# Scan groups in pairs on TensorE, one visit for the transposes of the decays, and smaller third and fourth weight loads in the first stage of a hybrid encoder layer

## The chip, the cores and the metric

The kernel runs on one core of one Trainium2 chip. The metric is the device time of one execution in microseconds (us), and lower is better. The kernel before takes 1320.09 us, the median of three runs (1319.91 to 1320.91). One further execution was taken under the profiler; its rows are what this document argues from.

A core has five engines with a queue each. TensorE (PE in the rows, PEld for its weight loads) multiplies matrices, VectorE (DVE) and ScalarE (ACT) do elementwise work, GpSimd (POOL) does elementwise work on SBUF alone, and SyncE (SP) issues most DMAs. Each engine takes its instructions in the order in which the program holds them and stops at one whose semaphores are not there yet. A releaser in the profile is the instruction or the transfer whose semaphore ended a wait.

## What is computed

One layer of a streaming encoder for 288 tokens (256 of a new stream, 32 of a running one) and a model width of 2048, all in float32. Cut to what matters here:

```python
xn   = rmsnorm(x, norm_mix_pre)
proj = xn @ w_in            # [u_pool 1024 | z 2048 | xBC 2560 | dt 32]
xbc  = silu(causal_dwconv(xbc))          # xs 2048, B and C 2 x 128 each
dt   = softplus(dt_raw + dt_bias); a = dt * A
# scan, 32 heads of 64 channels, state 128:
lmat   = exp(where(causal, acum_l - acum_s, -inf))
y_diag = einsum('bcgls,bcgjls,bcsgjp->bcgljp', C @ B.T, lmat, xs * dt)
y      = y_diag + (C @ h_prev) * exp(acum) + D * xs
y      = y * silu(z);  y = y * rsqrt(mean(y * y) per group + eps) * ssd_norm
x = x + rmsnorm(concat[pool, y] @ w_out, norm_mix_post)
x = x + rmsnorm(ConvFFN(rmsnorm(x, norm_ffn_pre)), norm_ffn_post)
```

The outputs are the two token groups and the new states (pool history, convolution histories, scan state).

## The kernel before

Activations lie with features on the 128 partitions and the 288 tokens along the row. The weights stream from memory once, in `raw` tiles (four buffers). Each piece of them is split in two: ACT makes `whi` (L129, in the first stage L276), a rounded copy in the reduced-precision type that TensorE reads fast, and DVE makes `wlo`, what the rounding left (L130, in the first stage L277). Four pieces of each are held. `mm3` (L135 to L137) then issues three matmuls of 128x128 weights by 288 tokens for each weight block: `whi` by the activation's high part, `whi` by its low part, `wlo` by its high part. These make up nearly all of TensorE's work. A project of 256 output columns over the 16 blocks of the model width is 16 x 2 x 3 = 96 such matmuls, fed by four pieces.

The stages that the change touches:

- First stage (L250 to L287). Six output blocks (B, C and the first two of xs) are made while x arrives. The weights `w_first` come from the SP queue in chunks of one, one, two, two, ... blocks of the model width (L251), the x tiles between them by the table `x_with`. `wdt` (the weights of dt), `par` and `hp`, `pc` and `pf` (parameters) are issued on the POOL queue at the chunks 1, 2 and 6. A chunk's buffer is free again when both ACT and DVE have read it.
- The decays (L355 to L417). From dt come `g` (accumulated decays), `dt` and `dec`, 32 heads on 32 partitions. For each of the three token blocks b, TensorE transposes g, dt and dec (L413 to L415) into a PSUM tile `ptok`, and DVE copies it to `tok` and `tokd` (L416, L417). The product of C and B (`pcb`, L430 to L432) follows.
- The scan (L442 to L485). `ssd_four(q)` handles four heads, q = 0 to 7: it loads `gb` (the decays broadcast to all partitions), `h0t` and `xw`; ACT makes `ce` (L453), `elast` (L454), twelve Relu activations into `m` with `tok` as bias (L464) and one Exp over m (L467); DVE scales `xw` (L459) and multiplies m by `cbt` (L469); TensorE runs 16 float32 matmuls into two PSUM tiles `py` (L476 to L482); DVE adds them to xs (L485). gb, h0t, xw, ce and m have two buffers each.
- The loops around it. Seven projects make the rest of xs, eight make z. After project i, `run_fours(n)` issues n groups by the tables XS_RATE and Z_RATE. `gate_rstd` (L487) sums squares with one float32 matmul `psum_g` (L489) and takes a root on ACT (L236), once after the fifth z project and once later.

PSUM has eight tiles: five under the tag `acc`, three under `aux`; `ptok`, `pcb`, `py` and `psum_g` are aux tiles, the projects use acc tiles two by two. The framework's scheduler orders each engine's instructions by readiness in its own timing model, so a group's matmuls need not stand where the tables ask for it; instructions under `tc.keep_in_program_order` keep their place.

Of the kernel before, what the change touches and what calls it, by code (L numbers as in the profile page):

```python
# [8 lines left out]
F32 = mybir.dt.float32  # L9
F32R = mybir.dt.float32r  # L10
AF = mybir.ActivationFunctionType
ALU = mybir.AluOpType
# [4 lines left out]
P = 128  # L17
# [4 lines left out]
NT = NP_ + NS  # L22
# [3 lines left out]
HEADS = 32  # L26
D_FF = 5632
EPS = 1e-6
KD = D_MODEL // P
NX = D_SSD // P  # L30
# [5 lines left out]
HALF = NF // 2  # L36
MW = 416
EVAC = 100
XS_RATE = (0, 0, 0, 1, 0, 1, 0, 1)
Z_RATE = (1, 0, 1, 0, 1, 1, 1, 0)  # L40


@with_exitstack
def body(
# [25 lines left out]
    act, dve, pool, pe, sp = nc.scalar, nc.vector, nc.gpsimd, nc.tensor, nc.sync  # L70
# [7 lines left out]
    acc_ps = ctx.enter_context(tc.tile_pool(name="acc_ps", bufs=5, space=PSUM))  # L78
# [3 lines left out]
    def aux(shape, name):  # L82
        return aux_ps.tile(shape, F32, tag="aux", name=name)
# [84 lines left out]
    def blocks_out(d, t, src, pool_):  # L168
# [12 lines left out]
    mean = const.tile([P, P], F32, name="mean")  # L181
# [4 lines left out]
        out=tri, in_=tri, pattern=[[1, P]], compare_op=ALU.is_ge, fill=0.0, base=0, channel_multiplier=-1  # L186
# [61 lines left out]
    for i in range(9):  # L248
        tc.keep_in_program_order(pe.matmul(idle, mean, mean, start=True, stop=True))
    first = [acc_ps.tile([P, NT], F32, tag="acc", name="acc") if m < 5 else aux([P, NT], "acc_x") for m in range(6)]  # L250
    chunks = ((0, 1), (1, 1)) + tuple((k, 2) for k in range(2, KD, 2))  # L251
    x_with = {0: (1, 1), 1: (2, 2), 2: (4, 2), 4: (6, 3), 6: (9, 3), 8: (12, 4)}
    for kb, n in chunks:
        raw = wpool.tile([P, n, 768], F32, tag="raw", name="raw")
        sp.dma_start(out=raw, in_=w_first[:, kb : kb + n, :])
        if kb in x_with:
            input_tiles(*x_with[kb])
        if kb == 1:
            pool.dma_start(out=wdt, in_=w_dt)
        if kb == 2:  # L260
            pool.dma_start(out=par1, in_=par1_in)
            pool.dma_start(out=hp, in_=hp_in)
        if kb == 6:
            pool.dma_start(out=pc, in_=par2_in[:, :120])
            pool.dma_start(out=pf, in_=par2_in[:, 120:].rearrange("p (r t) -> p r t", r=6))
        for k in range(kb, kb + n):
            a = atile("xn")
            with ExitStack() as order:
                for ins in cut[k - 2] if k > 2 else ():
                    order.enter_context(tc.issue_after(ins.ins))  # L270
                split_from(a, xT[:, k, :], g_mix_pre[:, k : k + 1])
            xn.append(a)
            hi, lo = wtile("hi", 1, 768)[:, 0, :], wtile("lo", 1, 768)[:, 0, :]
            step = 256 if k == 0 else 768
            for c in range(0, 768, step):
                w_hi = act.activation(hi[:, c : c + step], raw[:, k - kb, c : c + step], AF.Copy)  # L276
# [131 lines left out]
    dec_s = mp.tile([HEADS, 4, NS], F32, name="dec_s")  # L408
    dve.tensor_copy(dec_s, dec[:, NP_:].unsqueeze(1).broadcast_to([HEADS, 4, NS]))
    dec_s = dec_s.rearrange("h r s -> h (r s)")  # L410
    for b, (go, o) in enumerate(((0, 0), (256, P), (288, NT - P))):
        p_ = aux([P, 3, HEADS], "ptok")
        pe.transpose(p_[:, 0, :], g[:, go : go + P], id32)  # L413
        pe.transpose(p_[:, 1, :], dt[:, o : o + P], id32)
        pe.transpose(p_[:, 2, :], dec_s if b == 2 else dec[:, o : o + P], id32)  # L415
# [23 lines left out]
    xs = []  # L439
    elast = const.tile([P, HEADS + 32], F32, name="elast")  # L440

    def ssd_four(q):  # L442
# [16 lines left out]
        dve.tensor_tensor(x4, x4, w, op=ALU.mult)  # L459
        m = mp.tile([P, 4, MW], F32, tag="m", bufs=2, name="m")  # L460
        for j in range(4):
            h = 4 * q + j
            for b, (lo_, hi_) in enumerate(((0, 256), (256, 384), (384, MW))):
                act.activation(  # L464
                    m[:, j, lo_:hi_], gb[:, j, lo_:hi_], AF.Relu, bias=tok[:, b, 0, h : h + 1], scale=-1.0
                )
        act.activation(m, m, AF.Exp, scale=-1.0)  # L467
        gi = q // 4
        dve.tensor_tensor(m, m, cbt[:, gi : gi + 1, :].broadcast_to([P, 4, MW]), op=ALU.mult)  # L469
        ys = [aux([P, NT], "py") for _ in range(2)]  # L470
        for k in range(4):
            for j in range(4):
                c = slice(64 * j, 64 * j + 64)
                y = ys[j // 2][64 * (j % 2) : 64 * (j % 2) + 64, :]
                if k == 0:
                    pe.matmul(y[:, 0:256], xw[:, 0, c], m[:, j, 0:256], start=True, stop=False)  # L476
                elif k == 1:
                    pe.matmul(y[:, 128:256], xw[:, 1, c], m[:, j, 256:384], start=False, stop=True)  # L478
                elif k == 2:
                    pe.matmul(y[:, 256:], xw[:, 2, c], m[:, j, 384:], start=True, stop=False)  # L480
                else:
                    pe.matmul(y[:, 256:], h0t[:, c], ce[:, j, :], start=False, stop=True)  # L482
        for i in range(2):
            t = 2 * q + i
            dve.scalar_tensor_tensor(xs[t], xs[t], dcol[:, t : t + 1], ys[i], op0=ALU.mult, op1=ALU.add)  # L485

    def gate_rstd(t):  # L487
        p_ = aux([P, NT], "psum_g")
        pe.matmul(p_, mean, gsum[t], start=True, stop=True)  # L489
# [48 lines left out]
    rg = []  # L538

    def run_fours(n):  # L540
        for _ in range(n):
            if fours and 2 * fours[0] + 1 < len(xs):
                q = fours.pop(0)
                ssd_four(q)
                done[0] = 2 * q + 1

    def run_gates():
        while gates and gates[0] in zs and gates[0] <= done[0]:
# [23 lines left out]
    run_fours(NX)  # L572
    run_gates()
    assert not gates and not fours

# [666 lines left out]
```

## Time and profile before

| | us |
|---|---|
| median of three runs | 1320.09 |
| the profiled execution, its own time | 1319.88 |
| its span in the trace | 1317.9 |
| TensorE busy | 1310.9 |
| VectorE busy | 894.7 |
| ScalarE busy | 670.9 |
| GpSimd busy | 232.6 |

The span runs from the first to the last profiled instruction; 2.0 us of the execution lie around it. The granted TensorE clock is 0.999 of full speed over the span. A row of the timeline gives the start in us from the span's start, the duration, engine, source line, operation, and tile written <- tiles read; rows of like instructions are merged with their count, and idle time before an instruction stands in brackets with its releaser. TensorE's matmuls are pipelined: a row lasts 0.29 us while the next starts 0.13 us later, so cost is read from one start to the next. A float32 matmul appears as two records, so x32 is 16 matmuls.

### The profile page before, as it was taken

The numbers are of one execution on the slowest core, as the hardware profiler recorded it, in microseconds if no ns is written. First come the engines' busy times: TensorE is split into PE (matmuls) and PEld (weight loads), VectorE is DVE, ScalarE is ACT, GpSimd is POOL, SyncE is SP. The second block draws the span as 40 slices with busy tenths as digits, with TensorE's granted clock in tenths as the row PEclk, the third lists the DMA queues.
The fourth block names the chain that finished last, engine by engine and source line by source line (L and its number), as shares of the span: only waits on it lengthen the run. The fifth ranks groups of instructions, "written<-read, shape, count | busy, mean of one in ns | idle before, by whom it ended". The sixth has DMA issues, their size and how long they took to land.

```text
span 1317.9 us, 25200 instructions
## 1 busy us (share of the span) xinstructions
PE 1310.9 (99%) x10067; PEld 1298.6 (99%) x10067; DVE 894.7 (68%) x1486; ACT 670.9 (51%) x1010; POOL 232.6 (18%) x368
## 2 busy tenths in 40 slices
PE   9999999999999999999999999999999999999998
PEld 9999999999999999999999999999999999999997
DVE  7999997779654599967766743346666666664544
ACT  7558876446543466644444433334444444444443
POOL 7321221221430200211211200001111111101110
PEclk9999999999999999999999999999999999999999
DMA  8668874465665556666544445455544554466663
GB/s 327 200 206 280 277 233 144 150 227 205 203 211 192 180 169 221 185 185 194 172 165 160 156 172 173 155 177 180 173 161 164 177 172 160 163 235 187 204 178 110
DMA packets 104068, 249.81 MB, mean 190 GB/s; under 512 B 64064, under 2 KB 69504, under 8 KB 81680
## 3 DMA queue, kind: packets, MB, share of 16 engines
q1 hardware_dynamic: 101584, 242.72, 56.0%
q0 software_dynamic: 1936, 5.31, 1.4%
q8 instruction: 78, 1.28, 0.4%
q14 instruction: 38, 0.31, 0.1%
q10 hardware_dynamic: 432, 0.19, 0.1%
HBM read 236.23 MB, written 11.95 MB: 188 GB/s over the span
## 4 chain that ended last, share of the span: by engine, by line
PE 99%; DMA 1%; ACT 0%; SPq 0%; issue 0%; DVE 0%
PE acc L135 31%; PE acc L137 31%; PE acc L136 31%; PE py L476 1%; PE acc_x L135 1%; PE acc_x L137 1%; PE acc_x L136 1%; DMA raw<-in_w_first 1%; PE pst L773 0%; PE run_a L1114 0%; PE low L1112 0%; PE run_b L1127 0%; PE py L478 0%; PE pdt L297 0%; PE py L482 0%; PE py L480 0%
## 5 line engine op out<-in xcount | busy, mean ns | idle before, releaser
L130 DVE TENSOR_TENSOR wlo<-raw,whi 128x1024 fp32r<-128x1024 f32 (+1 forms) x386 | 463.0, 1201 | 313.2 <-ACT whi L129 310.7
L129 ACT ACTIVATE whi<-raw 128x1024 fp32r<-128x1024 f32 (+1 forms) x386 | 400.2, 1038 | 463.3 <-PE acc L136 370.5
L135 PE MATMUL acc<-hn,whi 128*128 128x288 f32 x1360 | 393.3, 294 | 0.0
L136 PE MATMUL acc<-hn,whi 128*128 128x288 f32 x1360 | 392.7, 293 | 0.0
L137 PE MATMUL acc<-hn,wlo 128*128 128x288 f32 x1360 | 391.9, 293 | 0.0
L135 PEld LDWEIGHTS acc<-hn,whi 128*128 128x128 f32 x1360 | 253.3, 188 | 0.4 <-ACT hn L873 0.4
L136 PEld LDWEIGHTS acc<-hn,whi 128*128 128x128 f32 x1360 | 253.3, 188 | 0.1
L137 PEld LDWEIGHTS acc<-hn,wlo 128*128 128x128 f32 x1360 | 253.3, 188 | 0.0
L135 PE MATMUL acc<-xn,whi 128*128 128x288 f32 x688 | 202.5, 296 | 0.7 <-ACT whi L276 0.7
L136 PE MATMUL acc<-xn,whi 128*128 128x288 f32 x688 | 200.3, 293 | 0.0
L137 PE MATMUL acc<-xn,wlo 128*128 128x288 f32 x688 | 195.0, 295 | 0.0
L135 PE MATMUL acc<-fa,whi 128*128 128x288 f32 x660 | 194.0, 294 | 0.0
L136 PE MATMUL acc<-fa,whi 128*128 128x288 f32 x660 | 193.4, 293 | 0.0
L137 PE MATMUL acc<-fa,wlo 128*128 128x288 f32 x660 | 193.1, 293 | 0.0
L135 PEld LDWEIGHTS acc<-xn,whi 128*128 128x128 f32 x688 | 129.3, 188 | 2.6 <-ACT whi L276 1.2
L136 PEld LDWEIGHTS acc<-xn,whi 128*128 128x128 f32 x688 | 129.2, 188 | 0.4
L137 PEld LDWEIGHTS acc<-xn,wlo 128*128 128x128 f32 x688 | 126.5, 188 | 0.0
L135 PEld LDWEIGHTS acc<-fa,whi 128*128 128x128 f32 x660 | 124.1, 188 | 0.0
L137 PEld LDWEIGHTS acc<-fa,wlo 128*128 128x128 f32 x660 | 123.9, 188 | 0.0
L136 PEld LDWEIGHTS acc<-fa,whi 128*128 128x128 f32 x660 | 123.9, 188 | 0.0
L925 POOL COPY fc_stage<-ebuf 128x4 f32<-128x4 f32 x88 | 27.7, 315 | 513.7 <-DVE ebuf L924 513.7
L921 POOL COPY ebuf<-pf 128x2 f32<-128x2 f32 x88 | 75.5, 858 | 129.5 <-DVE fc L931 83.0
(312 smaller groups left out, 1742.2 us busy)
## 6 DMA issues: line engine op xcount, KB each, us to landing
raw<-in_w_up SPq DMA_DIRECT2D x80, 1024.0 KB, 4.8
raw<-in_w_in SPq DMA_DIRECT2D x38, 1024.0 KB, 5.0
raw<-in_w_down SPq DMA_DIRECT2D x32, 1024.0 KB, 4.8
raw<-in_w_out SPq DMA_DIRECT2D x23, 1024.0 KB, 4.8
raw<-in_w_down SPq DMA_DIRECT2D x16, 768.0 KB, 4.3
raw<-in_w_up SPq DMA_DIRECT2D x8, 896.0 KB, 4.5
gb<-g_d SPq DMA_DIRECT2D x8, 832.0 KB, 6.2
raw<-in_w_first SPq DMA_DIRECT2D x7, 768.0 KB, 10.0
```

The source lines that it names most:

```text
L129: act.activation(hi, raw[:, k : k + n, :], AF.Copy)
L130: dve.tensor_tensor(lo, raw[:, k : k + n, :], hi.bitcast(F32), op=ALU.subtract)
L135: pe.matmul(out, wh, a[:, 0, :], start=start, stop=False)
L136: pe.matmul(out, wh, a[:, 1, :], start=False, stop=False)
L137: pe.matmul(out, wl, a[:, 0, :], start=False, stop=stop)
L476: pe.matmul(y[:, 0:256], xw[:, 0, c], m[:, j, 0:256], start=True, stop=False)
L921: pool.tensor_copy(e[:, 258:260], pf[:, 4:6, i])
L925: pool.tensor_copy(fc_stage[:, :, :, i], e[:, 256:324].rearrange("p (s c) -> p s c", c=34)[:, :, 0:2])
```

## The change

First stage: the chunks of `w_first` become 1, 1, 1, 1, 2, 2, ... blocks; `wdt`, `par` and `hp` are issued on the SP queue behind the chunk and x tile of kb = 8, `pc` and `pf` behind kb = 10. Decays: one PSUM tile holds all three token blocks; nine transposes stand together in a fixed order, and two DVE copies replace six. Scan: `ssd_four` is cut in `four_in` (loads, ACT and DVE work) and `four_out` (matmuls and the addition to xs). `run_fours(2)` runs both `four_in`, then both `four_out` with their 32 matmuls in a fixed order, the first of them issued after the second group's product m. The fourth `py` tile is an acc tile. The rates become one pair at a time: behind the last xs project and behind the z projects 2, 4 and 6 (counted from 0). The first `gate_rstd` moves ahead of the pair behind z project 4, its matmul pinned.

```diff
-XS_RATE = (0, 0, 0, 1, 0, 1, 0, 1)
-Z_RATE = (1, 0, 1, 0, 1, 1, 1, 0)
+XS_RATE = (0, 0, 0, 0, 0, 0, 0, 2)
+Z_RATE = (0, 0, 2, 0, 2, 0, 2, 0)
...
-    chunks = ((0, 1), (1, 1)) + tuple((k, 2) for k in range(2, KD, 2))
+    chunks = ((0, 1), (1, 1), (2, 1), (3, 1)) + tuple((k, 2) for k in range(4, KD, 2))
...
-        if kb == 1:
-            pool.dma_start(out=wdt, in_=w_dt)
-        if kb == 2:
-            pool.dma_start(out=par1, in_=par1_in)
-            pool.dma_start(out=hp, in_=hp_in)
-        if kb == 6:
-            pool.dma_start(out=pc, in_=par2_in[:, :120])
-            pool.dma_start(out=pf, in_=par2_in[:, 120:].rearrange("p (r t) -> p r t", r=6))
+        if kb == 8:
+            sp.dma_start(out=wdt, in_=w_dt)
+            sp.dma_start(out=par1, in_=par1_in)
+            sp.dma_start(out=hp, in_=hp_in)
+        if kb == 10:
+            sp.dma_start(out=pc, in_=par2_in[:, :120])
+            sp.dma_start(out=pf, in_=par2_in[:, 120:].rearrange("p (r t) -> p r t", r=6))
...
-    for b, (go, o) in enumerate(((0, 0), (256, P), (288, NT - P))):
-        p_ = aux([P, 3, HEADS], "ptok")
-        pe.transpose(p_[:, 0, :], g[:, go : go + P], id32)
-        pe.transpose(p_[:, 1, :], dt[:, o : o + P], id32)
-        pe.transpose(p_[:, 2, :], dec_s if b == 2 else dec[:, o : o + P], id32)
-        dve.tensor_copy(tok[:, b, :, :], p_[:, 0:2, :])
-        dve.tensor_copy(tokd[:, b, :], p_[:, 2, :])
+    def tok_out():
+        p_ = aux([P, 3, 3, HEADS], "ptok")
+        jobs = [(2, 2, dec_s)] + [(b, 2, dec[:, P * b : P * b + P]) for b in range(2)]
+        for b, (go, o) in enumerate(((0, 0), (256, P), (288, NT - P))):
+            jobs += [(b, 0, g[:, go : go + P]), (b, 1, dt[:, o : o + P])]
+        for n, (b, i, src) in enumerate(jobs):
+            ins = pe.transpose(p_[:, b, i, :], src, id32)
+            if n:
+                tc.keep_in_program_order(ins)
+        dve.tensor_copy(tok, p_[:, :, 0:2, :])
+        dve.tensor_copy(tokd, p_[:, :, 2, :])
...
+    def four_out(q, ys, xw, h0t, ce, m, _, after=None):
...
+        for y, w_, v_, go, end in ops:
+            with ExitStack() as order:
+                if after is not None:
+                    order.enter_context(tc.issue_after(after.ins))
+                ins = pe.matmul(y, w_, v_, start=go, stop=end)
+            tc.keep_in_program_order(ins)
+            after = None
...
     def run_fours(n):
...
+        got = [four_in(q) for q in qs]
+        ys = [aux([P, NT], "py") for _ in range(3)] + [acc_ps.tile([P, NT], F32, tag="acc", name="py_a")]
+        for i, q in enumerate(qs):
+            four_out(q, ys[2 * i : 2 * i + 2], *got[i], after=None if i else got[-1][-1])
+        done[0] = 2 * qs[-1] + 1
...
+        if i == 4:
+            assert gates[0] >= 8
+            rg.append(gate_rstd(0, True))
         run_fours(Z_RATE[i])
...
-        if i == 4:
-            assert gates[0] >= 8
-            rg.append(gate_rstd(0))
```

How the built programs differ in order, at three places. First TensorE where the decays are transposed, before: a first part of the transposes as they stand among the projection's matmuls (two more such places follow 32 and 46 rows on, with `dec` and `dec_s`, and `pcb` after those).

```order
L137 MATMUL acc<-xn,wlo 128x288
L413 MATMUL ptok<-ident,g 128x32
L414 MATMUL ptok<-ident,dt 128x32
L135 MATMUL acc<-xn,whi 128x288
L413 MATMUL ptok<-ident,g 128x32
L414 MATMUL ptok<-ident,dt 128x32
L413 MATMUL ptok<-ident,g 128x32
L414 MATMUL ptok<-ident,dt 128x32
L136 MATMUL acc<-xn,whi 128x288
```

And the same place now: the last of the nine transposes and `pcb`.

```order
L416 MATMUL ptok<-ident,dec_s 128x32
L416 MATMUL ptok<-ident,dec 128x32 x2
L416 MATMUL ptok<-ident,g 128x32
L416 MATMUL ptok<-ident,dt 128x32
...
L435 MATMUL pcb<-bc 128x256
```

Where TensorE left the projection four times for transposes and a fifth time for `pcb`, it now leaves it once. In the same way the nine visits for `py` become four, and `py` and `psum_g` at z project 4 stay one visit.

Second, ACT around the first root, before: the Relu activations of a group, then the table of the root, the root, one `whi`, and the table for Exp.

```order
L464 ACTIVATE m<-gb,tok 128x32
L236 ACT_TABLE_LOAD
L236 ACTIVATE rg<-psum_g,eps_t 128x288
L500 ACTIVATE sq<-xs 128x288
L129 ACTIVATE whi<-raw 128x1024
L467 ACT_TABLE_LOAD
L467 ACTIVATE m<-m 128x1664
```

Now:

```order
L533 ACTIVATE tanh_z<-z 128x288
L129 ACTIVATE whi<-raw 128x1024
L236 ACT_TABLE_LOAD
L236 ACTIVATE rg<-psum_g,eps_t 128x288
L533 ACT_TABLE_LOAD
L533 ACTIVATE tanh_z<-z 128x288
L469 ACTIVATE m<-gb,tok 128x256
```

The root now stands behind one `whi` and its table load, and ahead of the next pair's Relu activations. TensorE's third `py` tile of that visit (first tile of the pair's second group) is the PSUM buffer that `psum_g` held, so that group's first matmul waits for the root.

Third, the SP queue of the first stage, before and now, from the third x load on.

```order
L225 DMA xT<-in_x 128x576
L255 DMA raw<-in_w_first 128x1536
L225 DMA xT<-in_x 128x576
L255 DMA raw<-in_w_first 128x1536
L225 DMA xT<-in_x 128x864 x2
L255 DMA raw<-in_w_first 128x1536
L225 DMA xT<-in_x 128x1152
L255 DMA raw<-in_w_first 128x1536 x4
```

```order
L225 DMA xT<-in_x 128x576
L255 DMA raw<-in_w_first 128x768
L225 DMA xT<-in_x 128x576
L255 DMA raw<-in_w_first 128x768
L225 DMA xT<-in_x 128x864 x2
L255 DMA raw<-in_w_first 128x1536
L225 DMA xT<-in_x 128x1152
L259 DMA wdt<-in_w_dt 128x512
L260 DMA par_119<-in_par 128x248
L255 DMA raw<-in_w_first 128x1536
L261 DMA hp<-in_hp 32x2
```

The chunk of blocks 4 and 5 now stands behind the two x loads of 864 columns, where it stood ahead of them; `wdt` and `par` stand in the SP queue ahead of the chunk of blocks 6 and 7.

More of the change, by code (lines that the diff above doesn't have):

```diff
@@ L410, in body @@
     dec_s = dec_s.rearrange("h r s -> h (r s)")
-    for b, (go, o) in enumerate(((0, 0), (256, P), (288, NT - P))):
-        p_ = aux([P, 3, HEADS], "ptok")
-        pe.transpose(p_[:, 0, :], g[:, go : go + P], id32)
-        pe.transpose(p_[:, 1, :], dt[:, o : o + P], id32)
-        pe.transpose(p_[:, 2, :], dec_s if b == 2 else dec[:, o : o + P], id32)
-        dve.tensor_copy(tok[:, b, :, :], p_[:, 0:2, :])
-        dve.tensor_copy(tokd[:, b, :], p_[:, 2, :])
+    def tok_out():
[9 more added lines that the diff above has]
+        dve.tensor_copy(tokd, p_[:, :, 2, :])
+    tok_out()
     bc = []
@@ L440, in body, with four_in @@
     elast = const.tile([P, HEADS + 32], F32, name="elast")
-    def ssd_four(q):
+    def four_in(q):
         c = slice(2 * P * q, 2 * P * q + 2 * P)
@@ L468, in ssd_four @@
         gi = q // 4
-        dve.tensor_tensor(m, m, cbt[:, gi : gi + 1, :].broadcast_to([P, 4, MW]), op=ALU.mult)
-        ys = [aux([P, NT], "py") for _ in range(2)]
+        got = dve.tensor_tensor(m, m, cbt[:, gi : gi + 1, :].broadcast_to([P, 4, MW]), op=ALU.mult)
+        return xw, h0t, ce, m, got
+    def four_out(q, ys, xw, h0t, ce, m, _, after=None):
+        ops = []
         for k in range(4):
@@ L475, in ssd_four @@
                 if k == 0:
-                    pe.matmul(y[:, 0:256], xw[:, 0, c], m[:, j, 0:256], start=True, stop=False)
+                    ops.append((y[:, 0:256], xw[:, 0, c], m[:, j, 0:256], True, False))
                 elif k == 1:
-                    pe.matmul(y[:, 128:256], xw[:, 1, c], m[:, j, 256:384], start=False, stop=True)
+                    ops.append((y[:, 128:256], xw[:, 1, c], m[:, j, 256:384], False, True))
                 elif k == 2:
-                    pe.matmul(y[:, 256:], xw[:, 2, c], m[:, j, 384:], start=True, stop=False)
+                    ops.append((y[:, 256:], xw[:, 2, c], m[:, j, 384:], True, False))
                 else:
-                    pe.matmul(y[:, 256:], h0t[:, c], ce[:, j, :], start=False, stop=True)
+                    ops.append((y[:, 256:], h0t[:, c], ce[:, j, :], False, True))
+        for y, w_, v_, go, end in ops:
[5 more added lines that the diff above has]
+            after = None
         for i in range(2):
@@ L485, in ssd_four, with gate_rstd @@
             dve.scalar_tensor_tensor(xs[t], xs[t], dcol[:, t : t + 1], ys[i], op0=ALU.mult, op1=ALU.add)
-    def gate_rstd(t):
+    def gate_rstd(t, pin=False):
         p_ = aux([P, NT], "psum_g")
-        pe.matmul(p_, mean, gsum[t], start=True, stop=True)
+        ins = pe.matmul(p_, mean, gsum[t], start=True, stop=True)
+        if pin:
+            tc.keep_in_program_order(ins)
         o = const.tile([P, NT], F32, tag="spread", bufs=3, name="rg")
@@ L540, in run_fours @@
     def run_fours(n):
[L541 to L545, printed above, removed]
+        qs = [fours.pop(0) for _ in range(n) if fours]
+        if not qs:
+            return
+        assert 2 * qs[-1] + 1 < len(xs)
+        got = [four_in(q) for q in qs]
[3 more added lines that the diff above has]
+        done[0] = 2 * qs[-1] + 1
     def run_gates():
```

1 line of the change is left out of this document (removed).

## The prediction

> **What bounds the kernel now.** I read the page first (busy times, then the chain that ended last), after that the timeline of TensorE at the places that the change touches, then ScalarE, VectorE and the queues there.
>
> ```profile
> PE 1310.9 (99%) x10067; PEld 1298.6 (99%) x10067; DVE 894.7 (68%) x1486; ACT 670.9 (51%) x1010; POOL 232.6 (18%) x368
> PE 99%; DMA 1%; ACT 0%; SPq 0%; issue 0%; DVE 0%
> ```
>
> TensorE is busy for 1310.9 of 1317.9 us and carries 99% of the chain, so no other engine has anything to give. A change gains only by what TensorE issues, by what it loses where it leaves one kind of matmul for another, or by one of its few stalls. The number of multiplications stays the same here, so I price the leaving (a "visit" below) and the stalls.
>
> **The visits.** TensorE's timeline at a whole group, at half a group (the other half, behind a further projection matmul, costs the same), and at a single transpose:
>
> ```profile
> 144.25 0.29 PE L136 MATMUL acc<-xn,whi 128*128 128x288 f32 x1
> 144.38 0.29 PE L137 MATMUL acc<-xn,wlo 128*128 128x288 f32 x1
> 144.61 1.08 PE L476 MATMUL py<-m,xw 128*64 128x256 f32 x8
> ...
> 146.74 0.29 PE L136 MATMUL acc<-xn,whi 128*128 128x288 f32 x1
> ```
>
> ```profile
> 125.96 0.29 PE L135 MATMUL acc<-xn,whi 128*128 128x288 f32 x1
> 126.18 0.65 PE L476 MATMUL py<-m,xw 128*64 128x256 f32 x4
> ...
> 127.43 0.29 PE L137 MATMUL acc<-xn,wlo 128*128 128x288 f32 x1
> ```
>
> ```profile
> 106.38 0.29 PE L135 MATMUL acc<-xn,whi 128*128 128x288 f32 x1
> 106.60 0.24 PE L415 MATMUL ptok<-ident,dec_s 32*128 32x32 f32 x1
> 106.77 0.40 PE L136 MATMUL acc<-xn,whi 128*128 128x288 f32 x1
> 107.01 0.30 PE L137 MATMUL acc<-xn,wlo 128*128 128x288 f32 x1
> ```
>
> Projection matmuls start 0.13 us apart (144.25 to 144.38). Each stretch from the last one ahead of a visit to the second one behind it holds two such steps. The whole group therefore costs 146.74 - 144.38 - 0.26 = 2.10 us beyond the projection, the half 127.43 - 125.96 - 0.26 = 1.21. Two halves are 2.42 for the same 16 matmuls, so one visit costs 2.42 - 2.10 = 0.32 by itself. Bounds: what is seen at the two edges of the half (0.22 instead of 0.13 going in, 0.24 instead of 0.13 coming back) is 0.20; the transpose's whole excess, its own work included, is 107.01 - 106.38 - 0.26 = 0.37. I take 0.32, the only one of the three that comes from equal work.
>
> Before, TensorE leaves the projection nine times for py, four for ptok, once for pcb and once for the later psum_g alone; the first psum_g follows a py group. After, the order has one visit for the nine transposes with pcb, four for the pairs (the first psum_g at the head of the third), and the later psum_g. That is 15 against 6: nine fewer, 9 x 0.32 = **2.8 us gained**, bounds 1.8 and 3.3. The transposes, the 128 matmuls of the scan and the two sums are as many as before. Four DVE copies fewer are worth nothing on the chain, since TensorE works beside them.
>
> **The first stage.** TensorE's only stall over half a microsecond is here; the rows are of TensorE, ScalarE, SP, the DMA issues and the windows (us, then busy time of PE, PEld, DVE, ACT, POOL, the clock, DMA share, GB/s).
>
> ```profile
> 11.20 0.40 PE L135 MATMUL acc<-xn,whi 128*128 128x288 f32 x1 [0.73 <-ACT whi L276]
> 16.09 0.30 PE L135 MATMUL acc<-xn,whi 128*128 128x288 f32 x1
> ```
>
> ```profile
> 10.30 1.58 ACT L276 ACTIVATE whi<-raw 128x768 fp32r<-128x768 f32 x2 [1.68 <-DMA raw<-in_w_first]
> 14.21 1.59 ACT L276 ACTIVATE whi<-raw 128x768 fp32r<-128x768 f32 x2 [0.81 <-DMA raw<-in_w_first]
> ```
>
> ```profile
> 4.08 0.64 SPq L255 DMA_DIRECT2D raw<-in_w_first  x1
> 4.77 1.06 SPq L225 DMA_DIRECT2D xT<-in_x  x2
> 6.49 0.33 SPq L255 DMA_DIRECT2D raw<-in_w_first  x1
> ```
>
> ```profile
> xT<-in_x SPq DMA_DIRECT2D x1, 432.0 KB, 11.0
> 0.00:14.20 14.20, 12.26 (x76) 11.77 (x77) 7.90 (x13) 8.84 (x18) 8.86 (x39) 1.00 0.88 312
> 2.00:20.00 18.00, 17.27 (x119) 16.78 (x118) 13.13 (x19) 13.31 (x30) 12.68 (x33) 1.00 1.02 382
> q0 software_dynamic: 272, 0.72, 3.7%
> ```
>
> Blocks 2 and 3 arrive as one load and reach ScalarE at 10.30; TensorE waited 0.73 for the first cast. At 382 GB/s half of that load (0.39 MB) is 1.0 us. Block 2 alone is thus there 1.0 us sooner, which covers the 0.73 with 0.3 over; block 3 is wanted a block's 18 matmuls (2.4 us) later and lands 1.0 later. **Gain 0.73.** Late next is the load of blocks 4 and 5. It was issued at 4.08, ahead of the two 432 KB loads of x; it now stands behind them and needs the buffer of block 0, which came free at 6.49. TensorE wants block 4 at 16.09 - 0.73 = 15.36, so its load by about 14.5 (one cast, 0.8, ahead). It landed at 14.21, when 14.2 us x 312 GB/s = 4.43 MB had come in. What now must come first is smaller: x up to tile 11 (12 x 0.147 MB), four single blocks (1.57) and the load itself (0.79), 4.13 MB, with POOL's 0.7 MB of parameters (queue q0, the first 50 us) out of the way. The 0.3 MB left are 0.8 us for whatever runs beside it; before, 4.43 - 3.24 - 0.7 = 0.5 MB of later loads did so (3.24 being what SP had queued up to that load), which would put it at 14.7, 0.2 late. If the 0.58 MB of the last x tiles and as much again of parameters run beside it, it is (4.13 + 1.16 - 4.43)/0.382 = 2.3 us later than 14.21, 2.0 late. **I take a net 0.5**, bounds +0.73 and 0.73 - 2.0 = -1.3.
>
> **The new wait.** At z project 4 the third py tile uses the PSUM buffer of psum_g and waits for the root on ScalarE. Behind it on TensorE stand 16 pinned matmuls and the whole projection. ScalarE and TensorE before:
>
> ```profile
> 213.82 1.08 PE L476 MATMUL py<-m,xw 128*64 128x256 f32 x8
> ...
> 215.71 0.75 PE L489 MATMUL psum_g<-gsum,mean 128*128 128x288 f32 x2
> 216.09 0.51 PE L135 MATMUL acc<-xn,whi 128*128 128x288 f32 x1
> ```
>
> ```profile
> 213.86 1.06 ACT L129 ACTIVATE whi<-raw 128x1024 fp32r<-128x1024 f32 x1
> ...
> 219.56 1.28 ACT L236 ACT_TABLE_LOAD   x1
> 220.85 0.50 ACT L236 ACTIVATE rg<-psum_g,eps_t 128x288 f32<-128x288 f32 x1
> ```
>
> From psum_g's start TensorE has 0.38 (215.71 to 216.09) and the first group's 1.89 (213.82 to 215.71) to do, 2.27 us. ScalarE, by the order, has one `whi`, the table and the root: 1.06 + 1.28 + 0.50 = 2.84 when that `whi` starts with the visit, as the one at 213.86 did. The wait is 0.57; if the `whi` or the table was taken up earlier, it is nothing. **I take 0.4 lost**, bounds 0 and 0.6; a root that comes as late as before is a rival.
>
> In the section "What ACT_TABLE_LOAD costs" of its page "ScalarE: Activation LUTs" the Trainium skill adds a drain of about 1380 ns to the load's 1283. By that rule the wait would be an estimated 1.4 us longer and the time 1318.4. The trace here speaks against it: the load at 219.56 lasts 1.28, and the root starts at 220.85, directly behind.
>
> **Sum:** -2.8 - 0.5 + 0.4 = -2.9 on the profiled execution's 1319.88 gives **1317.0 us**; that execution lies 0.2 under the median, within the runs' spread. The bounds give 1315.9 (3.3 + 0.73) and 1320.0 (1.8 gained, 1.3 and 0.6 lost), all the bad ends together; the forecast's own range is 1315.9 to 1318.2.
>
> **The rivals.** All that bunching does falls on ScalarE and VectorE, since a pair's 32 matmuls are pinned and stop TensorE until both products are there. Window and groups, 144 to 246 us:
>
> ```profile
> 144.00:246.00 102.00, 102.00 (x875) 98.94 (x874) 89.72 (x144) 69.38 (x128) 19.64 (x17) 1.00 0.66 206
> L464 ACT ACTIVATE m<-gb,tok 128x256 f32<-128x256 f32 x16 | 8.0, 498 | 1.2 <-PE py L480 1.2
> L467 ACT ACTIVATE m<-m 128x1664 f32<-128x1664 f32 x4 | 6.4, 1589 | 0.0
> L464 ACT ACTIVATE m<-gb,tok 128x128 f32<-128x128 f32 x16 | 6.2, 388 | 0.0
> L464 ACT ACTIVATE m<-gb,tok 128x32 f32<-128x32 f32 x16 | 4.9, 308 | 0.0
> L129 ACT ACTIVATE whi<-raw 128x1024 fp32r<-128x1024 f32 x30 | 31.5, 1055 | 13.8 <-PE acc L136 12.1 <-issue 1.7
> L469 DVE TENSOR_TENSOR m<-m,cbt 128x1664 f32<-128x1664 f32 x5 | 10.0, 2003 | 0.3 <-ACT m L467 0.3
> L459 DVE TENSOR_TENSOR xw<-xw,tok 128x768 f32<-128x768 f32 x4 | 3.8, 953 | 1.6 <-DMA xw<-xs_d 1.6
> L485 DVE SCALAR_TENSOR_TENSOR xs<-xs,par,py 128x288 f32<-128x288 f32 x10 | 4.7, 506 | 0.0
> ```
>
> *ScalarE's chain eats the gain.* m has two buffers, so a pair's Relus start when the pair ahead has left them. Two z projects are 192 x 0.13 = 25.2 us. A group is (8.0 + 6.2 + 4.9 + 6.4)/4 = 6.4 on ScalarE, the pair 12.8, then 2.0 on VectorE. Eight `whi` (8.4) and ScalarE's other work, (69.38 - 31.5 - 25.5) x 25.2/102 = 3.1, make 26.3 if all goes ahead of the products. That is 1.1 late at the visits behind z projects 4 and 6, 2.2 in all: 1317.0 + 2.2 = **1319.2**. For it: the sum exceeds the gap. Against it: nothing makes all the `whi` stand ahead, ScalarE stood idle 13.8 us for `whi` here, mostly for buffers, and neighbouring rows overlap.
>
> *VectorE becomes the bound (slower).* Before, it was busy 89.72 of these 102 us with four groups' products and the end of a fifth. With m's two buffers only one pair can be done when the first pair's visit comes, 233 projection matmuls behind the transposes at 106.4, so near 106.4 + 233 x 0.13 + 2 = 139 us; thus six groups fall between it and the last visit. Two more are 2 x (2.0 + 0.95 + 1.0) = 8.0, 97.7 of 102 busy. If VectorE keeps its idle time of 12.3, it needs 110, 8 too many, and `wlo` (behind which TensorE's third matmuls wait) comes late. It decides from 2.9 of them on, when the gain is used up; the middle between 2.9 and 8 is 5.5, **1322.5**. For it: the 97.7. Against it: the idle time was spent on releases that a fuller queue covers, and the gating of xs and z can lag without stopping TensorE.
>
> *Block 4 late.* At the bad bound 1.8 of the gain is lost: **1318.8**. For it: its later issue. Against it: fewer bytes ahead.
>
> *The root as late as before.* It started 220.85 - 215.71 = 5.1 us after psum_g and would end 5.6 after; less 2.27 that is 3.4 instead of 0.4: **1320.0**. Against it: the Relus that preceded it then stand behind it now.
>
> **How the numbers follow.** A difference under 0.2% (2.6 us) can't be told from none here. Forecast 55%, ScalarE's chain 17%, VectorE 16%, block 4 7%, the root 5%. Faster by over 0.2% means under 1317.45: 48 of the forecast's 55 and 2 of ScalarE's, 50%. Slower: 15 of VectorE's and 1 of ScalarE's, 16%. The rest, 34%, is within 0.2%. The range is 1315.9 to 1320.8: it holds the forecast's own and three rivals, and leaves VectorE's case and a few per cent below.
>
> **What would show it.** Right: TensorE's busy time with idle rows falls, six visits with one pair near 4.2 - 0.3 = 3.9 us, no bracket at block 2, a bracket of 0 to 0.6 with root L236 as releaser at the third pair. Wrong: brackets by `m` ahead of the py rows (ScalarE's chain), by `wlo` on the third matmuls between 140 and 240 us (VectorE), by L276 near 15 us (block 4), or a pair that costs 4.2 (no price on visits). A pair's `gb` landing late would look like the first and isn't priced.

## The result: slower by 0.18%, and the profile after

Measured side by side on one chip, 18 runs each, the changed kernel takes 1323.06 us (median; 1320.43 to 1326.88) and the kernel before 1320.37 (1319.59 to 1323.24). The ratio is 1.0018, with a 95% interval of 1.0012 to 1.0024. The forecast was 1317.0. The profiled execution took 1322.52 with a span of 1320.5. Its page, busy times and the chain that ended last:

```profile
PE 1310.2 (99%) x10067; PEld 1298.2 (98%) x10067; DVE 892.9 (68%) x1482; ACT 671.9 (51%) x1010; POOL 227.4 (17%) x363
PE 89%; DVE 4%; DMA 3%; ACT 2%; issue 1%; SPq 1%; DVEq 0%; ACTq 0%
```

TensorE is busy 0.7 us less than before, but the span is 2.6 us longer: work was saved and waits came in. The chain, 99% TensorE before, now runs through VectorE, transfers and ScalarE for a tenth of its length. What TensorE waited for (us in total, times, longest) in the changed kernel:

```profile
PE acc L137 <- DVE wlo L130: 2.4, 3, 1.4
PE idle L249 <- POOL mean L182: 1.2, 1, 1.2
PE acc L135 <- ACT whi L275: 0.7, 1, 0.7
PE y_ps L1178 <- ACT diag L1177: 0.6, 1, 0.6
PE psum_g L505 <- POOL gsum L519: 0.4, 1, 0.4
PE py L496 <- ACT rg L236: 0.4, 1, 0.4
```

The waits for `mean` and `diag` were there before. `whi` at L275 is the first stage's stall, as long as before (0.73, now 0.66) and elsewhere. New are three waits for `wlo`, and one each at psum_g and at the root.

The visits cost what was forecast. A pair, in TensorE's timeline:

```profile
140.34 0.29 PE L136 MATMUL acc<-xn,whi 128*128 128x288 f32 x1
140.47 0.29 PE L137 MATMUL acc<-xn,wlo 128*128 128x288 f32 x1
140.69 1.73 PE L496 MATMUL py<-m,xw 128*64 128x256 f32 x24
...
144.59 0.30 PE L136 MATMUL acc<-xn,whi 128*128 128x288 f32 x1
```

144.59 - 140.47 - 0.26 = 3.86, against 2 x 2.10 = 4.20 for two groups apart, and 3.9 forecast.

Where the 2.5 us came from is seen by counting projection matmuls (from 0, those of the first stage included) in both timelines and comparing the time at which the same one starts. The table holds points at which both kernels have done the same other work:

| projection matmul | changed minus before, us | what lies between |
|---|---|---|
| 254, late in the first stage | +0.34 | first stage (0.17 of it stands at the very first matmul) |
| 671, last ahead of the transposes | +0.34 | nothing |
| 745, behind the transposes and `pcb` | -0.62 | the joined visit: 0.96 gained |
| 1634, behind the last group | +2.53 | the scan: 3.15 lost |
| 1900 | +2.53 | nothing |

The scan should have gained 1.6 here (five visits). It lost 3.15, so its waits come to some 4.7. From one start to the next, the three waits for wlo cost 1.1, 0.5 and 1.6 us, 3.25 together (the brackets show less, since a matmul behind a wait is slow as well). psum_g and the root cost 1.3; 0.2 stays unplaced.

VectorE ahead of the three late `wlo`, and the matmul that waited first, in the changed kernel:

```profile
122.24 0.48 DVE L171 STREAM_TRANSPOSE blocks<-xs 128x288 f32<-128x288 f32 x1 [3.23 <-DMA xs_d<-blocks]
122.64 1.85 DVE L474 TENSOR_TENSOR m<-m,cbt 128x1664 f32<-128x1664 f32 x1
124.41 1.22 DVE L130 TENSOR_TENSOR wlo<-raw,whi 128x1024 fp32r<-128x1024 f32 x1
```

```profile
125.68 0.40 PE L137 MATMUL acc<-xn,wlo 128*128 128x288 f32 x1 [0.82 <-DVE wlo L130]
```

```profile
153.25 0.96 DVE L464 TENSOR_TENSOR xw<-xw,tok 128x768 f32<-128x768 f32 x1 [2.79 <-DMA xw<-xs_d]
...
154.96 1.85 DVE L474 TENSOR_TENSOR m<-m,cbt 128x1664 f32<-128x1664 f32 x1
156.73 1.22 DVE L130 TENSOR_TENSOR wlo<-raw,whi 128x1024 fp32r<-128x1024 f32 x1
...
196.84 0.96 DVE L464 TENSOR_TENSOR xw<-xw,tok 128x768 f32<-128x768 f32 x1 [2.27 <-DMA xw<-xs_d]
197.72 1.89 DVE L474 TENSOR_TENSOR m<-m,cbt 128x1664 f32<-128x1664 f32 x1
199.52 3.58 DVE L130 TENSOR_TENSOR wlo<-raw,whi 128x1024 fp32r<-128x1024 f32 x2
```

The picture on VectorE is the same three times: it stands still for a transfer of the scan, then does a group's product, and only then the `wlo` that TensorE is short of. At the second and third place ScalarE was late as well. The rows are two neighbouring `whi` each time, with the pair's Relus and other work between them:

```profile
140.67 1.06 ACT L129 ACTIVATE whi<-raw 128x1024 fp32r<-128x1024 f32 x1 [0.65 <-PE acc L136]
...
152.27 1.05 ACT L129 ACTIVATE whi<-raw 128x1024 fp32r<-128x1024 f32 x1
...
183.64 1.04 ACT L129 ACTIVATE whi<-raw 128x1024 fp32r<-128x1024 f32 x1
...
197.07 1.05 ACT L129 ACTIVATE whi<-raw 128x1024 fp32r<-128x1024 f32 x1
```

The second and the fourth ended at 153.32 and 198.12, so with ScalarE as it ran, and no stop on VectorE, the two `wlo` could have started at most 3.4 and 1.4 us sooner. VectorE's totals show no shortage of time. Its window 144 to 246 us (columns as in the prediction):

```profile
144.00:246.00 102.00, 99.66 (x843) 96.56 (x840) 88.70 (x141) 76.29 (x151) 16.49 (x15) 1.00 0.69 220
```

VectorE is busy 88.70 of 102 us, less than the 89.72 of before; the VectorE rival counted on 97.7. Part of the difference is work that fell out of the window: it holds six products, as the rival counted, but 29 `wlo` (36.6 us) instead of 31 (38.4 us). The idle time was 13.3 us all the same. ScalarE has more to do, 76.29 against 69.38.

The third pair's visit shows the wait that the prediction had priced, and one that it hadn't (TensorE, then ScalarE):

```profile
213.45 0.29 PE L137 MATMUL acc<-xn,wlo 128*128 128x288 f32 x1
214.11 0.75 PE L505 MATMUL psum_g<-gsum,mean 128*128 128x288 f32 x2 [0.37 <-POOL gsum L519]
...
217.12 0.65 PE L496 MATMUL py<-m,xw 128*64 128x256 f32 x4 [0.36 <-ACT rg L236]
```

```profile
214.21 1.04 ACT L129 ACTIVATE whi<-raw 128x1024 fp32r<-128x1024 f32 x1
215.27 1.28 ACT L236 ACT_TABLE_LOAD   x1
216.56 0.50 ACT L236 ACTIVATE rg<-psum_g,eps_t 128x288 f32<-128x288 f32 x1
```

ScalarE did `whi`, table and root in a row as forecast. `whi` ended at 214.21 + 1.04 = 215.25, right ahead of the table load, and the root followed the load directly once more (215.27 + 1.28 = 216.55). The drain of about 1380 ns that the Trainium skill adds to the load (page "ScalarE: Activation LUTs", section "What ACT_TABLE_LOAD costs") isn't seen here either, ahead of the load or behind it. psum_g, first in the visit now, waited for GpSimd's sum `gsum`.

### The profile page after: what moved, and what is told of

The parts are those of the page before. It is cut to its first block, busy times and chain, and to the rows that moved or that the text cites. A ratio compares the mean times of both kernels' runs of the same rounds, so it can differ in the third digit from the quotient of the medians.

```text
span 1320.5 us, 25189 instructions
## 1 busy us (share of the span) xinstructions
PE 1310.2 (99%) x10067; PEld 1298.2 (98%) x10067; DVE 892.9 (68%) x1482; ACT 671.9 (51%) x1010; POOL 227.4 (17%) x363
## 3 DMA queue, kind: packets, MB, share of 16 engines
q8 instruction: 78, 1.28, 0.4%
## 4 chain that ended last, share of the span: by engine, by line
PE 89%; DVE 4%; DMA 3%; ACT 2%; issue 1%; SPq 1%; DVEq 0%; ACTq 0%
PE acc L137 28%; PE acc L135 28%; PE acc L136 28%; DVE wlo L130 1%; DMA raw<-in_w_first 1%; DMA xw<-xs_d 1%; DMA xs_d<-blocks 1%; ACT whi L129 1%; PE acc_x L135 1%; PE acc_x L137 1%; PE acc_x L136 1%; DVE conv L346 1%; ACT m L469 1%; SPq L174 0%; DMA g_d<-g 0%
## 5 line engine op out<-in xcount | busy, mean ns | idle before, releaser
L952 DVE SCALAR_TENSOR_TENSOR fc<-ebuf,pf,fc 128x290 f32<-128x290 f32 x176 | 90.1, 517 | 2.6
```

The costliest lines, as they stand in the source:

```text
L952: dve.scalar_tensor_tensor(c, e[:, r_ : r_ + 290], pf[:, r_, i : i + 1], c, op0=ALU.mult, op1=ALU.add)
```

## Experiments

Three theories were set against each other. **A**: VectorE takes its queue in order and stands behind transfers of the scan for which a pair leaves no time. **B**: VectorE has too much work between the visits. **C**: a pair's Relus and Exps stand ahead of `whi` on ScalarE. In the expectations of e1 to e3 the letters A and B stand for theories of their own, which they state. An edit also makes the scheduler order the rest anew, so no run differs from its neighbour in one row alone; for that reason a control (e9) is among them. Times are medians; before was run on the same chip each time: 1320.12 beside e1 to e4, 1320.72 beside e5 to e8, 1320.25 beside e9 to e12. Runs beside different ones of these are compared by their distance from their own before; for the changed kernel that is +2.7 us.

| run | us | ratio to before (95%) |
|---|---|---|
| e1 first stage alone | 1320.19 | 1.0001 (0.9992 to 1.0009) |
| e2 transposes alone | 1321.75 | 1.0018 (1.0010 to 1.0027) |
| e3 changed, first stage of before | 1322.94 | 1.0021 (1.0012 to 1.0031) |
| e4 changed, 4 xw and 2 blocks buffers | 1324.88 | 1.0032 (1.0020 to 1.0044) |
| e5 changed, 2 blocks buffers | 1321.31 | 1.0017 (1.0002 to 1.0031) |
| e6 changed, xw scaled on GpSimd, 2 blocks | 1318.85 | 0.9985 (0.9977 to 0.9994) |
| e7 changed, second group held back | 1318.32 | 0.9979 (0.9970 to 0.9988) |
| e8 changed, xw scaled on GpSimd | 1324.40 | 1.0027 (1.0017 to 1.0038) |
| e9 before, xw on GpSimd, 2 blocks | 1320.56 | 1.0003 (0.9994 to 1.0011) |
| e10 transposes, xw on GpSimd, 2 blocks | 1319.42 | 0.9994 (0.9985 to 1.0003) |
| e11 as e7, first stage of before | 1318.52 | 0.9986 (0.9977 to 0.9996) |
| e12 all cures, psum_g elsewhere | 1318.07 | 0.9981 (0.9972 to 0.9990) |

### The parts of the change (e1, e2, e3, e11)

**e1** is the kernel before with the change's first-stage hunk (chunks and parameters), nothing else.

> The kernel before with the first stage's edit alone (single blocks for 2 and 3, parameters on the SP queue behind the chunks). Theory A (the edit moves the stall and does not remove it: in the changed kernel's trace the wait of 0.73 us at block 2 has gone and one of 0.66 us stands at block 4, and TensorE reaches projection matmul 671 0.34 us later than before): the median is 0.2 to 0.5 us over the kernel before, with the same bracket at block 4. Theory B (the prediction's step, a net gain of 0.5; what the changed kernel showed was one unlucky landing): 0.3 to 0.7 us under it.

It measured no difference, though its interval (-1.1 to +1.2 us) doesn't shut out the forecast 0.5 either. The bracket at block 4 that its theory A expected wasn't there; TensorE waited 0.76 at the start of the projection (5.63 us) and 0.57 at block 6 (21.02 us). **e3** is the changed kernel with that hunk undone:

> The changed kernel with the first stage of before: pairs and transposes alone. Theory A (the first stage's edit costs 0.3 us, everything else of the loss is in the scan): 0.3 us under the changed kernel, so 2.0 to 2.4 us over before, with the same three waits for wlo and the two at psum_g and the root. Theory B (the first stage's edit, by what it does to later transfers, makes the waits for wlo): they vanish, and the time is 1 to 2 us under before.

2.8 us over its before, level with the changed kernel's 2.7, and the waits remain; of those for `wlo`, two came back (0.4 and 1.0 us). **e11** asks the same in a kernel without waits for wlo (its base, e7, is below):

> The changed kernel with the second group of a pair held back (2.4 us faster than before), with the first stage of before put back: the first stage's edit by itself, in a kernel that has no waits for wlo which could hide it. If the edit gains the predicted 0.5: this run is 0.5 us slower than with it. If it costs the 0.34 of the changed kernel's trace: 0.3 us faster. If the stall only moves: within 0.3 us.

It is 1.7 us faster than its before, where e7 is 2.4 faster than its own: 0.7 apart on the side of a gain, but the ratios' intervals overlap. Over all the profiles here, TensorE's start of matmul 254 against the profile of before lies at -0.31 to +0.34 (mean 0.0, eight profiles) with the edit and at -0.09 to +0.51 (mean 0.2, six profiles with that of before) without. The first stage's end thus varies by 0.6 us from one execution to the next whichever way it is loaded, and the +0.34 of the table above is one draw from that. The means differ by 0.2 in the edit's favour, which is inside that scatter. Whether the stall shrinks a little or only moves stays open.

**e2** is the kernel before with the change's `tok_out` alone.

> The kernel before with the nine transposes in one visit alone. Theory A (a visit costs 0.3 us by itself and four of them go): 1.0 to 1.3 us faster, no new wait. Theory B (a visit has no price of its own; the pieces only looked dear because they were small): within 0.3 us of the kernel before.

Both theories missed. TensorE gained 1.0 us up to matmul 800 (119 us), as A says. Then it lost 2.1 in two waits that A had excluded, almost 100 us later. What TensorE waited for:

```profile
PE acc L137 <- DVE wlo L130: 1.7, 2, 1.0
```

VectorE there had no transfer ahead of `wlo`. On ScalarE twelve Relus stood between one `whi` (190.38) and the next (197.16):

```profile
190.38 1.04 ACT L129 ACTIVATE whi<-raw 128x1024 fp32r<-128x1024 f32 x1
...
192.67 1.90 ACT L470 ACTIVATE m<-gb,tok 128x256 f32<-128x256 f32 x6
194.48 0.29 ACT L459 ACTIVATE ce<-gb 128x128 f32<-128x128 f32 x1
194.68 1.91 ACT L470 ACTIVATE m<-gb,tok 128x256 f32<-128x256 f32 x6
...
197.16 1.04 ACT L129 ACTIVATE whi<-raw 128x1024 fp32r<-128x1024 f32 x1
```

and behind it, on VectorE, a product of 2.50 us ahead of a `wlo`. Joining the transposes had changed ScalarE's and VectorE's order in all that follows. The kernel before holds an order in which TensorE never waits for `wlo`; a rebuilt one need not.

### Cures for the waits (e4 to e8)

**e4** and **e5** give the tiles that VectorE waited for more buffers.

```diff
-        s = pool_.tile([P, NT], F32, tag="blocks", bufs=1, name="blocks")
+        s = pool_.tile([P, NT], F32, tag="blocks", bufs=2 if pool_ is mixer_pool[0] else 1, name="blocks")
...
-        xw = mp.tile([P, 3, 2 * P], F32, tag="xw", bufs=2, name="xw")
+        xw = mp.tile([P, 3, 2 * P], F32, tag="xw", bufs=4, name="xw")
```

(e5 without the second edit.)

> The changed kernel with four buffers for xw instead of two and two for the scan's blocks tile instead of one; nothing else is edited. Theory A (VectorE stands in order behind transfers that a pair leaves no time for: it sat idle 3.23 us for the store of blocks, 2.79 and 2.27 us for the load of xw, each time ahead of the product m and of the wlo that came late): the three waits for wlo (3.2 us of TensorE's time) shrink to under 1 us, the time is 2 to 3 us under the changed kernel, level with before. Theory B (VectorE has too much work between the pairs' visits): VectorE's work is the same, the waits stay, within 0.5 us of the changed kernel. Theory C (ScalarE makes whi late because a pair's Relus and Exps stand ahead of it): the waits stay too, and the last idle time of VectorE before them names whi.

> The changed kernel with two buffers for the scan stage's blocks tile, xw left at two (the run with both had moved much of the order and was slower). Theory A (VectorE stands in order behind transfers): the wait for wlo near 125 us, which had VectorE idle 3.23 us for the store of blocks ahead of it, goes; those near 158 and 201, behind loads of xw, stay or shrink with the stores that the queue has sooner: 1 to 2.5 us under the changed kernel. Theory C (a pair's Relus and Exps on ScalarE make whi late): no change beyond 0.5 us.

e4 went against all three: 4.8 us over its before, some 2 more than the changed kernel. More buffers let the loads be issued sooner, but VectorE still waited 7.2 us for xw, five times, and one wait for wlo grew to 2.04; the wait at the root grew to 1.6. In its trace e5 did what A says of it: the wait near 125 went, one behind a load of xw (3.39 us idle on VectorE) stayed, and TensorE stood 1.07 us. Its time doesn't settle the matter: its runs spread from 1319.31 to 1327.49, which the section on the hardware takes up, so that its median is 0.6 over its before, but its ratio, 1.0017, is no lower than the changed kernel's 1.0018.

**e6** and **e8** take the load of xw out of VectorE's queue:

```diff
-        dve.tensor_tensor(x4, x4, w, op=ALU.mult)
+        pool.tensor_tensor(x4, x4, w, op=ALU.mult)
```

e6 has the two blocks buffers as well.

> The changed kernel with the scaling of xw (8 x 0.95 us) on GpSimd instead of VectorE, and two buffers for blocks. VectorE's queue then has neither of the two waits for a transfer in it; a pair's work on ScalarE is bunched as before. Theory A: all waits for wlo (3.2 us) go, those at psum_g and the root (1.3) stay, no clock drop: 3 us or more under the changed kernel, 0 to 1.5 us under before. Theory C: the waits stay, within 0.7 us of the changed kernel.

> The changed kernel with the scaling of xw on GpSimd alone, blocks left at one buffer. Theory A: the waits for wlo near 158 and 201 us (behind xw, 1.6 and 0.5 us of TensorE's time) go, the one near 125 (behind the store of blocks, 1.1) stays: 1.5 to 2.5 us under the changed kernel. Theory C: within 0.7 us of the changed kernel.

e6 is 1.9 us faster than before, and TensorE waits for no `wlo`:

```profile
PE idle L251 <- POOL mean L184: 1.2, 1, 1.2
PE y_ps L1181 <- ACT diag L1180: 0.6, 1, 0.6
PE py L499 <- ACT rg L238: 0.4, 1, 0.4
PE acc L135 <- ACT whi L277: 0.3, 1, 0.3
```

The wait for xw is now GpSimd's, 17.5 us of it in five times, and costs nothing there. e8, without the second buffer, was slower than the changed kernel. The transfer left over had become the costlier one; what VectorE waited for in e8, 100 to 250 us:

```profile
DVE blocks L171 <- DMA xs_d<-blocks: 13.3, 5, 5.0
DVE m L474 <- ACT m L472: 5.5, 2, 2.8
```

Its four waits for wlo sum to 4.2. Three of them, near 122, 128 and 160 us, stand behind such a stop (2.65, 2.33 and 5.05 us). At the fourth, near 204, the product ahead of `wlo` waited 2.66 us for ScalarE's Exp, with no transfer in it. A alone doesn't explain that one.

**e7** leaves buffers and engines as they are and breaks the bunch. `his` collects the activations that make `whi`; the second group's instructions come behind the first of the four that belong to the z project (or last xs project) ahead of the visit.

```diff
-        got = [four_in(q) for q in qs]
+        got = [four_in(qs[0])]
+        for q in qs[1:]:
+            with tc.issue_after(his[0-4].ins):
+                got.append(four_in(q))
```

> The changed kernel with the ScalarE, VectorE and load instructions of each pair's second group held back until whi of the first weight piece of the project ahead of the pair's visit has been issued; the visits and all tiles are as they were. Theory C (bunching on ScalarE): two groups no longer stand in one block ahead of whi, the waits for wlo shrink to under 1 us, 2 to 3 us under the changed kernel. Theory A (transfers at the head of VectorE's queue): the second xw is loaded later and its wait is as long or hidden by chance; at most 1 us is gained.

2.4 us faster than before, no wait for `wlo`. VectorE's one wait for xw is longer than any in the changed kernel, and it does no harm (e7's lines stand one or two further down, so `wlo` is L131):

```profile
190.68 0.96 DVE L465 TENSOR_TENSOR xw<-xw,tok 128x768 f32<-128x768 f32 x1 [4.80 <-DMA xw<-xs_d]
191.55 1.88 DVE L475 TENSOR_TENSOR m<-m,cbt 128x1664 f32<-128x1664 f32 x1
193.36 0.95 DVE L465 TENSOR_TENSOR xw<-xw,tok 128x768 f32<-128x768 f32 x1
194.23 1.22 DVE L131 TENSOR_TENSOR wlo<-raw,whi 128x1024 fp32r<-128x1024 f32 x1
```

That `wlo` ended at 195.45 and its first matmul started at 197.16, 1.7 us later. The `wlo` ahead of it had ended at 182.88, 11.1 us before its own first matmul at 194.02. So the stop and the group work ate 9.4 us of a lead and stayed just inside it. This lead, read for every piece between 105 and 250 us, is at least 2.7 us in the kernel before. In the changed kernel it swings between 12 us, which VectorE gains while TensorE is away at a pair, and nothing at the three waits. Its least is 0.8 in e6, 1.7 in e7 and 2.4 in e12 (below).

So neither A nor C is the whole cause. A `wlo` comes late when the stops for transfers and the bunched group work ahead of it together outlast its lead. In the changed kernel both stood there. e2 and the fourth wait of e8 had the bunch alone right ahead, and the first wait of e8 a stop without a product. Taking away transfers (e6) or spreading the group work (e7) was enough, but the two cures aren't cleanly apart: e7 also cut VectorE's stops for transfers between 112 and 250 us from 11.9 to 6.2 us, so A's share and C's share of the loss aren't shown. That a new order alone freed these kernels of waits isn't ruled out by any one run; against it, e3, e4, e5 and e8 were re-ordered too and kept theirs, and e6, e7, e11 and e12 have none. B falls as the whole cause: e6 takes 7.6 us of work off VectorE, but e7 takes off none.

### Control, and the best version (e9, e10, e12)

**e9** has e6's two edits on the kernel before; **e10** has them on e2.

> Control: the kernel before with the scaling of xw on GpSimd and two buffers for blocks, nothing of the change. TensorE of the kernel before waits for no wlo, so if these two edits act only by keeping wlo in time (theory A), they are worth nothing here: within 0.5 us of before. If they are worth 1 us or more by themselves (VectorE's or the queue's load as such), the gain of the changed kernel with them says nothing about the pairs.

> The joined transposes alone (1.6 us slower than before, though TensorE's trace had its gain of 1.0 us up to 120 us and lost 2.1 in two waits for wlo near 201 and 205 us), now with the scaling of xw on GpSimd and two buffers for blocks. Theory A (the waits come from what stands ahead of wlo in VectorE's queue): no wait for wlo, 0.8 to 1.3 us faster than before. Rival (joining the transposes makes all that follows late on ScalarE): the waits stay, slower than before by 1 us or more.

The edits are worth nothing by themselves (e9). With them the joined transposes bring 0.8 us in the median, though the interval just reaches no gain, and there is no wait for `wlo` in the trace, where TensorE gains 0.98 at the transposes. Against its before e10 stands 2.5 us better than e2: the visit's price is real, and the loss of e2 lay in the order of the rest. The rival, that joining makes all that follows late, is out.

**e12** joins e7 and e6 and moves the first psum_g behind z project 5, where no pair stands:

```diff
-        if i == 4:
-            assert gates[0] >= 8
-            rg.append(gate_rstd(0, True))
         run_fours(Z_RATE[i])
...
+        if i == 5:
+            rg.append(gate_rstd(0))
```

> All three cures together (second group held back, xw scaled on GpSimd, two blocks buffers), and the first psum_g behind z project 5, where no pair stands, so that no py tile waits for the root. Adding up: 0.32 us for one more visit, 0.7 to 1.3 us of waits at psum_g and the root gone, no waits for wlo: 2.6 to 3.2 us under before, about 1317.5, and no run with a lowered clock.

1318.07, 2.2 us under before and short of the 2.6 to 3.2 expected: the waits at psum_g and the root are gone from its trace, and its profiled execution, 1317.44, is the shortest one profiled. In the medians it can't be told from e7, whose 1318.32 came from another set of runs.

## Why the prediction was wrong

- **The visits** were right: 2.8 us forecast; 0.96 at the transposes and, from the pairs' 3.86, 8 x 2.10 + the halves' extra 0.32 - 4 x 3.86 = 1.7 in the scan, 2.6 together. Where the waits are cured, the time comes to 1318.3 (e7) against a forecast of 1317.0. In e7 the third pair's visit still lost 0.7 us (a bracket of 0.52 at the root): 2.6 - 0.7 = 1.9, and TensorE stood 2.1 ahead of before at matmul 1900 of its trace, 2.4 in the medians.
- **The first stage** isn't borne out in size: net 0.5 forecast, no difference clear of the noise measured (e1, e3, e11), with 0.5 not shut out. Block 2's stall went as forecast, and in the changed kernel's trace "block 4 late" took its place: ScalarE stood 2.45 us for that load and TensorE 0.66. The sum took one landing time to 0.1 us, where executions differ by 0.6.
- **The new wait** at the root came as forecast, with `whi`, table and root in a row. It was put at 0.4; with psum_g's own wait for `gsum`, which wasn't priced, the visit lost 1.3. Moving psum_g to the head of a pinned visit had taken GpSimd's sum onto the path.
- **The step that failed** is the one that settled what the pairs do to the other engines. It compared totals: VectorE's 97.7 of 102 us busy, ScalarE's 26.3 in a gap of 25.2, and dismissed the first with "the idle time was spent on releases that a fuller queue covers". VectorE's queue doesn't cover a release; it stands in it. VectorE stayed at 88.70 us busy and was late all the same. The forecast put waits for `wlo` at nothing; the three cost 3.25 us, more than the visits gained. "ScalarE's chain eats the gain" looked for the products at the py rows; those were always in time, and `wlo` behind them was not.
- **The VectorE rival** named the right bracket (`wlo` on the third matmuls) and gave 1322.5, near the 1322.52 profiled, but for a reason that the runs refute. Its agreement is chance.
- The transposes were priced as a local edit. e2 shows that they weren't: the scheduler's order changed everywhere behind them.

## What to carry to other kernels

Pricing a move of work between engines by busy totals isn't enough when queues are in order: list what would stand directly ahead of the instruction that the bound engine needs next, which transfer or bunch can stop there, and how far ahead of its use that instruction is done now. When a framework orders instructions by readiness in a model of its own, any edit re-deals the places at which such stops meet; a kernel at 99% on one engine has an order worth protecting, so feed the bound engine from a queue without transfers in it, or spread bunched work by hand, and then join visits. Take a gain of a few tenths at a place that varies by more from run to run as not measured.

## What the runs showed of the hardware

A wait can cost twice. In e8 TensorE waited 1.75 us for `wlo`; its timeline then:

```profile
119.98 0.29 PE L136 MATMUL acc<-xn,whi 128*128 128x288 f32 x1
122.02 0.40 PE L137 MATMUL acc<-xn,wlo 128*128 128x288 f32 x1 [1.75 <-DVE wlo L130]
...
122.80 0.44 PE L136 MATMUL acc<-xn,whi 128*128 128x288 f32 x1
123.04 0.44 PE L137 MATMUL acc<-xn,wlo 128*128 128x288 f32 x1
...
126.16 0.31 PE L135 MATMUL acc<-xn,whi 128*128 128x288 f32 x1
126.31 0.30 PE L136 MATMUL acc<-xn,whi 128*128 128x288 f32 x1
```

The granted clock in two windows of 1 us there (eighth column, behind the five busy times with their counts):

```profile
124.00:125.00 1.00, 1.00 (x6) 1.00 (x6) 0.27 (x1) 1.00 (x3) 0.00 (x0) 0.50 0.04 10
126.00:127.00 1.00, 1.00 (x9) 1.00 (x9) 1.00 (x2) 0.82 (x2) 0.00 (x0) 0.91 0.45 74
```

From 122.80 to 126.16, 3.4 us, the clock was at half and matmuls started 0.24 us apart instead of 0.13: 14 of them, 1.5 us lost on top of the wait. In e4 the same followed a wait of 2.04 (0.50 from 163 to 165); waits of 1.35 in the changed kernel, 1.62 in e4 and 1.68 in e8 left the clock at 1.00. In its page "TensorE: Matmul & The Clock Gate", section "What's actually happening", the Trainium skill gives a free-running window of 3413 ns, and the 3.4 us agree. In the section "HAM oscillation — how this bites in real kernels" of the same page the Trainium skill warns of idle gaps above some 3.4 us; here 1.75 us was enough, and the measurement decides.

This may be part of why the changed kernel's runs spread over 6.5 us. Of its 18 runs, nine had a mean granted clock of 0.998 or less; their median is 1324.43, that of the other nine 1321.46. e7 had none of eleven runs so, e5 four of eleven (1326.5 against 1320.0). Two things limit this reading. A mean of 0.998 alone is no proof: e11's profiled execution has it, with the clock at 1.00 from 6 to 1312 us and at half only at its end (0.50 from 1313 to 1317); six of the changed kernel's nine are lower, at 0.996 or 0.997. And the medians lie 3.0 us apart, where one stretch at half clock cost 1.5. Only the profiled executions have traces, and that of the changed kernel has no such stretch inside its work; one was seen in e4 and one in e8.
